# Layer 1's down-projection as seven products over both halves of the sequence, with its weights kept in SBUF

## The chip, the cores and the metric

One core of one Trainium2 chip. The metric is device time in microseconds (us) of one execution of the whole program; lower is better. The kernel before takes 2318.09 us, the median of 3 runs (2316.0 to 2323.02).

## What is computed

A trunk of two layers over a sequence of 1024 tokens of width 1024, then a final RMSNorm, all in float32. Layer 0 mixes with attention and spatial gating, layer 1 with a convolution. After each mixer comes a gated feed-forward, and the change is in the second of them:

```python
def conv_ffn(h, w_up, dw_w, dw_b, w_down):
    hh = causal_dwconv(h @ w_up, dw_w, dw_b)
    a, gate = jnp.split(hh, 2, axis=-1)
    return (a * jax.nn.silu(gate)) @ w_down
...
        x = x + conv_ffn(rms_norm(x, norm_ffn_g[l]), ffn_w_up[l], ffn_dw_w[l],
                         ffn_dw_b[l], ffn_w_down[l])
    return rms_norm(x, final_norm_g)
```

The hidden width is 2816, which is 22 tiles of 128. The down-projection of a layer is a product of 1024 tokens by 2816 by 1024.

## The kernel before

**Precision.** Every float32 operand of a matmul is split into a high and a low part (`split_hi_lo`, L138 to L144): ACT casts the high part (L140), POOL or DVE subtracts it for the low one (L144). Each product then takes three matmuls (`PASSES`, L157: high by high, high by low, low by high). A split operand is a buffer `hl` of 2 x 512 columns, of which the pool `whl` has 8; a raw operand of 1024 columns comes into one of 4 `raw` buffers (`wraw`).

**The sequence in two chunks.** Tokens are worked on in two chunks of 512 (`CH`). The residual stream of a chunk is one tile `xr` of 4 row tiles of 128.

**The up-projection** of a layer begins with plain products for the first hidden tiles (`head_steps`, L546), 8 of 22 in layer 1. Beside them `combos` (L578) makes sums and differences of the normed activations of both chunks. The other 14 tiles are made by `pair_steps` (L619): a step takes one hidden tile, its gate and its value, and computes both chunks' products with seven block products instead of eight (Strassen and Winograd's scheme, numbered 1 to 7; `product`, L638). A product is 12 matmuls. The seven weight operands of a step are sums of four quarters of weights, made by DVE (L662 to L665) and POOL (L667) and split by `part`. The products' banks are read by ACT copies (L676, L679, L682, L693) and DVE additions (L684, L686, L689) into rows `rg` and `rv_`; `conv` (L646) runs the width-3 convolution on each (ACT L648, two DVE operations L650), ACT applies SiLU (L691), and DVE multiplies value by gate (L695). The gated unit of 128 x 1024 goes to DRAM (`phd`).

**The down-projection** (`down_steps`, L699) is plain. Per chunk and per half of the output columns, 11 groups `dp` of two hidden tiles run: each loads 512 KB of weights and 512 KB of gated units from DRAM, splits both, and issues 24 matmuls (L721) into 4 banks, one for each row tile of 128 tokens; the last two groups run together, bank by bank, 12 matmuls each, and DVE adds each bank to `xr` (L726). That is 44 groups and 1056 matmuls for a layer. The weights are read twice, once for each chunk.

**The order.** Each engine runs its own list of instructions in order. The lists come from a scheduler that may place an instruction earlier or later than the program text, as long as its data allow. In layer 1 the text runs `ffn_rest`, then loads `xr`, then `down_steps(1, 0)`, then `down_steps(1, 1)` interleaved with `final_steps(0)` (the last norm of chunk 0, L955 to L983, whose POOL multiplication is L974), then `final_steps(1)`. Loads and stores go by SP's queue.

Of the kernel before, what the change touches and what calls it, by code (L numbers as in the profile page):

```python
# [10 lines left out]
F32 = mybir.dt.float32  # L11
# [9 lines left out]
P = 128  # L21
S = 1024
# [23 lines left out]
ROWS = 5  # L46
PRE0, PRE0_LATE = 6, 2
PRE1, PRE1_LATE = 8, 2
DP = HT // 2
# [7 lines left out]
def trunk_kernel(ctx: ExitStack, tc: tile.TileContext, x, norm_mix_g, norm_ffn_g, ab_w_in, ab_w_out,  # L57
# [43 lines left out]
    def run(steps):  # L101
        for f in steps:
            f()
# [213 lines left out]
    phd = [dram.tile([P, HT, S], F32, name=f"phd{l}") for l in range(2)]  # L317
# [227 lines left out]

    def head_steps(l, c, hT, js):  # L546
# [31 lines left out]
    def combos(l, hT, up_pool):  # L578
# [4 lines left out]
        def f(k):  # L583
# [6 lines left out]
            for c in range(2):  # L590
                t = c * TPC + k
                xt = up_pool.tile([P, D], F32, tag="row", name="xa", bufs=ROWS)
# [26 lines left out]
    def pair_steps(l, hT, T, js, up_pool):  # L619
# [34 lines left out]
        def f(j):  # L654
# [16 lines left out]
            a4 = part(v2, "pool")  # L671
            rg, rv_ = row(), row()
# [23 lines left out]
            nc.sync.dma_start(out=phd[l][:, j, :], in_=yv)  # L696
        return [lambda j=j: f(j) for j in js]

    def down_steps(l, c):  # L699
# [4 lines left out]
        def f(half, dp):  # L704
            if dp == 0:
# [3 lines left out]
                                                      in_=phd[l][:, 2 * dp:2 * dp + 2, c * CH:(c + 1) * CH]), PH_ENGINES)  # L709
# [19 lines left out]
    def x_from(src):  # L729
# [3 lines left out]
        return f  # L733

# [48 lines left out]
    def const_steps():  # L783
        rv = lambda ap: ap.rearrange("(c p) -> c p", p=P)

        def taps(c):
# [31 lines left out]
    def ffn_rest(l, hT, pre):  # L818
        with tc.tile_pool(name=f"up{l}", bufs=1) as up_pool:
            first, last, T = combos(l, hT, up_pool)  # L820
            interleave(head_steps(l, 1, hT, range(pre)), first, 0.0, 0.6)
            run(last)
            run(pair_steps(l, hT, T, range(pre, HT), up_pool))

# [106 lines left out]
    for c in range(NCH):  # L931
# [20 lines left out]
    for c in range(NCH):  # L952
        x_from(xd[1])(c)
# [31 lines left out]
    run(down_steps(1, 0))  # L985
    interleave(down_steps(1, 1), final_steps(0), 0.0, 0.5)
    run(final_steps(1))
# [36 lines left out]
```

## Time and profile before

| | before |
|---|---|
| median of 3 runs | 2318.09 us (2316.0 to 2323.02) |
| the profiled execution | 2318.01 us, its span 2316.3 us |
| mean granted TensorE clock | 0.970 |
| PE busy | 2171.3 us, 94% of the span |
| DVE, ACT, POOL busy | 1598.2, 1130.6, 1124.9 us |
| layer 1's products of the up-projection, on the chain that ended last | 1798.73 to 2055.62 us |
| layer 1's down-projection | from 2055.62 us to about 2304 us |

The rows further down come from the one profiled execution. Times are us from the start of its span; the mean of a group is in ns. A line such as L721 is a line of the kernel as printed above. A timeline's row gives start, length, engine, line and the operation's output and inputs; a group's row gives the count, the busy time, the mean of one, and the idle time of the engine just before them.

### The profile page before, as it was taken

The page shows a single profiled execution, that of the slowest core. Times are in us where ns is not written, and L with a number is a line of the kernel's source. Part 1 is how long each engine was busy: PE and PEld are TensorE (multiplying, and loading weights), DVE is VectorE, ACT ScalarE, POOL GpSimd, SP SyncE. Part 2 cuts the span into 40 slices and gives each one's busy share as a digit, 9 for nine tenths or more (in the row PEclk, how much of TensorE's full clock was granted, in tenths as well). Part 3 has the DMA queues.
Part 4 walks back from the last instruction along what each step waited for, and adds up shares of the span by engine and source line. Part 5 has one row for each costly group of instructions (what it writes and reads, how often), then busy time and mean ns, then how long its engine had stood idle before and what let it go on. Part 6 is the DMA issues. An engine that isn't in the chain of part 4 may idle for free.

```text
span 2316.3 us, 28698 instructions
## 1 busy us (share of the span) xinstructions
PE 2171.3 (94%) x10014; PEld 1781.0 (77%) x10014; DVE 1598.2 (69%) x2654; ACT 1130.6 (49%) x1993; POOL 1124.9 (49%) x879
## 2 busy tenths in 40 slices
PE   8888979989999999999999969979989999999997
PEld 6677758778788888878887758857768888888786
DVE  6675747964876666665599969996576666665654
ACT  4344525742544444544556566555433544544444
POOL 3312311222645444545579827974543554445554
PEclk9989979999999999999999979979989999999999
DMA  7736545435532222365534522522532222265564
GB/s 238 212 97 208 169 150 186 156 96 169 165 98 89 84 82 82 108 228 199 183 110 127 155 73 84 153 72 102 182 116 94 73 85 93 75 221 194 193 223 146
DMA packets 304049, 322.49 MB, mean 139 GB/s; under 512 B 12060, under 2 KB 221216, under 8 KB 303392
## 3 DMA queue, kind: packets, MB, share of 16 engines
q1 hardware_dynamic: 298016, 305.97, 41.1%
q0 software_dynamic: 5888, 14.68, 2.0%
q8 instruction: 79, 1.29, 0.2%
q14 instruction: 66, 0.54, 0.1%
HBM read 266.08 MB, written 54.53 MB: 138 GB/s over the span
## 4 chain that ended last, share of the span: by engine, by line
PE 70%; DVE 17%; issue 4%; ACT 3%; POOL 3%; DMA 2%; SPq 0%; ACTq 0%; DVEq 0%; POOLq 0%
PE bank L642 25%; PE bank L721 15%; PE bank L302 13%; PE bank L265 12%; DVE sbank L866 5%; DVE hl L144 2%; DVE y L178 2%; POOL ap L863 1%; PE sbank L461 1%; POOL hl L144 1%; DVE xn L193 1%; ACT hl L140 1%; PE sbank L209 1%; PE bank L430 1%; PE sbank L609 1%
## 5 line engine op out<-in xcount | busy, mean ns | idle before, releaser
L144 POOL TENSOR_TENSOR hl<-raw,hl 128x512 fp32r<-128x512 f32 x544 | 796.2, 1483 | 619.4 <-ACT hl L140 590.8
L140 ACT CAST hl<-raw 128x512 fp32r<-128x512 f32 x792 | 454.7, 617 | 339.2 <-PE bank L721 162.0
L302 PE MATMUL bank<-big,hl 128*128 128x512 f32 x2112 | 499.6, 395 | 9.0 <-DVE big L221 3.0
L721 PE MATMUL bank<-hl 128*128 128x512 f32 x2112 | 489.2, 391 | 8.3 <-DVE hl L144 6.5
L721 PEld LDWEIGHTS bank<-hl 128*128 128x128 f32 x2112 | 393.9, 188 | 98.9 <-DVE hl L144 15.2
L302 PEld LDWEIGHTS bank<-big,hl 128*128 128x128 f32 x2112 | 396.5, 190 | 94.8 <-ACT big L220 4.9
L265 PE MATMUL bank<-hl,big 128*128 128x512 f32 x1728 | 427.2, 401 | 20.5 <-POOL hl L144 9.3
L144 DVE TENSOR_TENSOR hl<-raw,hl 128x512 fp32r<-128x512 f32 x248 | 276.1, 1139 | 197.9 <-ACT hl L140 197.5
L265 PEld LDWEIGHTS bank<-hl,big 128*128 128x128 f32 x1728 | 325.6, 192 | 91.3 <-POOL hl L144 9.9
L642 PE MATMUL bank<-big,hl 128*128 128x512 f32 x1440 | 345.5, 390 | 0.1
L642 PEld LDWEIGHTS bank<-big,hl 128*128 128x128 f32 x1440 | 269.8, 188 | 59.0 <-POOL hl L144 1.0
L650 DVE SCALAR_TENSOR_TENSOR s<-row,dw,s 128x1024 f32<-128x1024 f32 x120 | 198.2, 1652 | 156.9 <-ACT s L648 153.0
L642 PE MATMUL bank<-t,hl 128*128 128x512 f32 x1080 | 265.3, 392 | 0.0
L866 DVE SCALAR_TENSOR_TENSOR sbank<-yb,cw,sbank 128x512 f32<-128x512 f32 x352 | 247.8, 746 | 6.0 <-ACT sbank L855 3.3
L642 PEld LDWEIGHTS bank<-t,hl 128*128 128x128 f32 x1080 | 202.5, 188 | 44.2
L863 POOL TENSOR_TENSOR ap<-ap,pr 128x512 f32<-128x512 f32 x112 | 154.2, 1376 | 35.3 <-ACT ap L858 21.5
L140 ACT CAST hl<-s 128x512 fp32r<-128x512 f32 x90 | 55.9, 621 | 156.9 <-DVE s L665 96.3
L556 DVE SCALAR_TENSOR_TENSOR s<-bank,dw,s 128x510 f32<-128x510 f32 x112 | 83.5, 745 | 57.0 <-ACT s L553 55.5
L862 ACT ACTIVATE pr<-yb,cw 128x512 f32<-128x512 f32 x112 | 80.8, 723 | 71.9 <-POOL ap L863 71.7
L667 POOL TENSOR_TENSOR s<-raw,s 128x512 f32<-128x512 f32 x30 | 38.9, 1295 | 122.8 <-DVE hl L144 122.7
L630 POOL MEMSET row<- 128x2 f32 x60 | 6.0, 99 | 156.4 <-DVE s L650 110.7
L648 ACT ACTIVATE s<-row,dw 128x1024 f32<-128x1024 f32 x60 | 74.9, 1248 | 12.2 <-DVE row L689 10.0
(170 smaller groups left out, 2082.8 us busy)
## 6 DMA issues: line engine op xcount, KB each, us to landing
raw<-in_ffn_w_up SPq DMA_DIRECT2D x116, 512.0 KB, 4.3
raw<-in_ffn_w_down SPq DMA_DIRECT2D x88, 512.0 KB, 3.8
raw<-phd SPq DMA_DIRECT2D x88, 512.0 KB, 4.7
raw<-in_ab_w_in SPq DMA_DIRECT2D x64, 256.0 KB, 4.0
raw<-in_conv_w_in SPq DMA_DIRECT2D x32, 512.0 KB, 4.0
phd<-s SPq DMA_DIRECT2D x30, 512.0 KB, 2.6
qd<-s SPq DMA_DIRECT2D x32, 256.0 KB, 2.8
qk<-qd POOLq DMA_DIRECT2D x8, 1024.0 KB, 7.1
```

The source lines that it names most:

```text
L140: nc.scalar.copy(out=hl_hi, in_=raw)
L144: eng.tensor_sub(out=hl_lo, in0=raw, in1=hl_hi.bitcast(F32))
L265: nc.tensor.matmul(ps, lhsT=hT[c][:, sa, d, tok(t)], rhs=units[d][:, sw, :], start=(n == 0), stop=(n == 3 * DT - 1))
L302: nc.tensor.matmul(ps, lhsT=hv[d // 4][:, sw, d % 4, :], rhs=hT[:, sa, d, :], start=(n == 0), stop=(n == 3 * DT - 1))
L556: nc.vector.scalar_tensor_tensor(out=y[:, sh:], in0=ps[:, :CH - sh], scalar=dw[:, k, ct:ct + 1], in1=y[:, sh:], op0=ALU.mult, op1=ALU.add)
L642: nc.tensor.matmul(ps, lhsT=hv[:, sw, d, :], rhs=B[n](sa, d), start=(start and i == 0), stop=(i == 11), skip_group_check=True)
L648: nc.scalar.activation(out=y, in_=r[:, 2:], func=AF.Identity, scale=dw[:, 2, ct:ct + 1], bias=dw[:, 3, ct:ct + 1])
L650: nc.vector.scalar_tensor_tensor(out=y, in0=r[:, k:k + S], scalar=dw[:, k, ct:ct + 1], in1=y, op0=ALU.mult, op1=ALU.add)
L721: nc.tensor.matmul(ps, lhsT=phs[i][:, sa, k * P:(k + 1) * P], rhs=wds[i][:, sw, :], start=(dp == 0 and n == 0), stop=(dp == DP - 1 and n = ...
L862: nc.scalar.activation(out=pr, in_=ys[ct][:, k:k + CH], func=AF.Copy, scale=cw[:, ct, k:k + 1])
L863: nc.gpsimd.tensor_add(out=st["ap"], in0=st["ap"], in1=pr)
L866: nc.vector.scalar_tensor_tensor(out=st["acc"], in0=ys[ct][:, k:k + CH], scalar=cw[:, ct, k:k + 1], in1=st["acc"], op0=ALU.mult, op1=ALU.add)
```

## The change

Layer 1's down-projection becomes `down_pair_steps`. Its hidden tiles are paired, `jj` with `HH + jj` (`HH` is 11). With the two chunks and the two column halves that makes blocks of 2 x 2 x 2, and each pair goes through the seven products. A product's unit for one pair is 3 matmuls for each of 4 row tiles: 12 matmuls, and 7 x 11 x 12 = 924 in all. Each of the four weight quarters of a pair (128 x 512) is loaded once and stays in SBUF, in `wraw`, in `big` and in a pool of its own; the weight operands of products 5, 3 and 7 are sums, for 3 and 7 made in place. The gated units' operands are kept in DRAM as seven slots `phs`. `sums` makes the three that are not plain, in the up-projection, as soon as both tiles of a pair exist; for this the pair steps go in the order k, HH + k, and the end of a pair (`finish`) is put into the next step, behind its weight splits. The products run in the order 2, 1, 5, 3, 6, 7, 4, into two sets of 4 banks, and at a product's end each bank is added to `xr` for each output block that it is part of. A next quarter's load is held back by a DVE copy of one element until a unit is made. In both layers the `row` buffers go from 5 to 4, and `combos` takes one of its two tiles from `s4`. Layer 0's down-projection stays plain.

```diff
-ROWS = 5
+ROWS = 4
...
+    def sums(jj, a11, a21, a12, a22):
...
+        nc.gpsimd.tensor_add(out=s1, in0=a21, in1=a22)
+        nc.gpsimd.tensor_sub(out=a21, in0=a11, in1=a21)
+        nc.gpsimd.tensor_sub(out=s2_, in0=s1, in1=a11)
+        s4_ = s2([P, CH])
+        nc.vector.tensor_sub(out=s4_, in0=a12, in1=s2_)
+        nc.sync.dma_start(out=phs[:, 4:6, jj, :], in_=sx)
+        nc.sync.dma_start(out=phs[:, 6, jj, :], in_=s4_)
...
             a4 = part(v2, "pool")
+            settle()
             rg, rv_ = row(), row()
...
-            nc.sync.dma_start(out=phd[l][:, j, :], in_=yv)
+            if l == 0:
+                nc.sync.dma_start(out=phd[:, j, :], in_=yv)
+            elif j < HH:
+                pair["a"] = yv
+            else:
+                pending.append(lambda: finish(j - HH, pair["a"], yv))
...
+        def weight(n, jj):
+            if n == 2:
+                place(jj)
+                load(2, jj)
+            (b11, b12), (b21, b22) = [(w[:, :512], w[:, 512:]) for w in W[jj]]
+            if n == 5:
+                t1 = s2([P, 512])
+                nc.vector.tensor_sub(out=t1, in0=b12, in1=b11)
+                return t1
+            if n == 3:
+                nc.gpsimd.tensor_sub(out=b12, in0=b22, in1=b12)
+                nc.vector.tensor_add(out=b11, in0=b11, in1=b12)
+            if n == 7:
+                nc.gpsimd.tensor_sub(out=b21, in0=b21, in1=b11)
+            return {3: b22, 2: b21, 1: b11, 6: b11, 7: b12, 4: b21}[n]
...
+            nc.sync.dma_start(out=raw[:, :len(js), :], in_=phs[:, SLOT[n], js[0]:js[-1] + 1, :])
+            us = []
+            for i, jj in enumerate(js):
+                us.append((unit(weight(n, jj), "pool"), unit(raw[:, i, :], "dve")))
+                if n in (2, 1, 5):
+                    load({2: 1, 1: 5, 5: 3}[n], jj, us[-1][1][:, 1, 0:1].bitcast(F32))
+            for grp in [us] if end else [[u] for u in us]:
+                for k in range(TPC):
...
+                    if end:
+                        for r, h in ADDS[n]:
+                            xt = xtile(r_tile(n, k))[:, h * 512:(h + 1) * 512]
+                            nc.vector.tensor_add(out=xt, in0=ps[k], in1=xt)
...
+        ds = down_pair_steps(1, dpool)
+        k = 5 * len(ds) // 7
+        run(ds[:2])
+        settle()
+        run(ds[2:4])
+        for c in range(NCH):
+            x_from(xd[1])(c)
+        run(ds[4:k])
+        interleave(ds[k:], final_steps(0), 0.0, 0.8)
+        run(final_steps(1))
```

The order of instructions on three lists, before and in the change. In the changed kernel L146 is the old L144, L663 is L630, L683 is L650, L695, L697, L698 and L700 are L662, L664, L665 and L667, L718, L720 and L723 are L684, L686 and L689, L729 is L695, and L1110 is L974. L553 to L557 are `sums`, L784 and L787 the in-place weight sums of products 3 and 7. A name with a number is one buffer.

DVE in the pair stage of layer 1, from the addition behind product 2 of one step to the weight sums of a later step, before:

```order
L689 TENSOR_TENSOR row<-bank,s_15737 128x512
L650 SCALAR_TENSOR_TENSOR s_15807<-row,dw_440,s_15807 128x1024 x2
L650 SCALAR_TENSOR_TENSOR s_15825<-row,dw_440,s_15825 128x1024
L662 TENSOR_TENSOR s_15977<-raw 128x512
L650 SCALAR_TENSOR_TENSOR s_15825<-row,dw_440,s_15825 128x1024
L664 TENSOR_TENSOR raw<-raw 128x512
L144 TENSOR_TENSOR hl<-s_15977,hl 128x512
L695 TENSOR_TENSOR s_15825<-s_15825,s_15807 128x1024
L684 TENSOR_TENSOR row<-bank,s_15907 128x512
L665 TENSOR_TENSOR s_15977<-s_15977,raw 128x512
```

and in the change, for the second tile of a pair:

```order
L723 TENSOR_TENSOR row<-bank,s_15634 128x512
L683 SCALAR_TENSOR_TENSOR s_15704<-row,dw_440,s_15704 128x1024 x2
L683 SCALAR_TENSOR_TENSOR s_15722<-row,dw_440,s_15722 128x1024 x2
L729 TENSOR_TENSOR s_15722<-s_15722,s_15704 128x1024
L557 TENSOR_TENSOR s_15762<-s_15722,sx 128x512
L723 TENSOR_TENSOR row<-bank,s_15785 128x512
L695 TENSOR_TENSOR s_15882<-raw 128x512
L697 TENSOR_TENSOR raw<-raw 128x512
L146 TENSOR_TENSOR hl<-s_15882,hl 128x512
L698 TENSOR_TENSOR s_15882<-s_15882,raw 128x512
```

The multiplication (old L695, now L729) was followed by the next step's split and additions, and the later step's weight sum (old L662) stood ahead of it. Now L557 stands right behind the multiplication, and behind L557 come a step's addition L723 and the weight sums L695 and L697 of the step after next.

POOL in the pair stage, before:

```order
L630 MEMSET row 128x2 x2
L667 TENSOR_TENSOR s_17113<-raw,s_17113 128x512
L144 TENSOR_TENSOR hl<-s_17113,hl 128x512
L144 TENSOR_TENSOR hl<-raw,hl 128x512 x3
L630 MEMSET row 128x2
```

and in the change:

```order
L700 TENSOR_TENSOR s_15731<-raw,s_15731 128x512
L146 TENSOR_TENSOR hl<-s_15731,hl 128x512
L146 TENSOR_TENSOR hl<-raw,hl 128x512 x4
L663 MEMSET row 128x2 x2
L553 TENSOR_TENSOR sx<-s_15581,s_15722 128x512
L554 TENSOR_TENSOR s_15581<-s_15581 128x512
L555 TENSOR_TENSOR sx<-sx,s_15581 128x512
L700 TENSOR_TENSOR s_15882<-raw,s_15882 128x512
L146 TENSOR_TENSOR hl<-s_15882,hl 128x512
```

The three sums L553 to L555 stand between the splits of one step and L700 of the step behind it.

POOL in the down-projection: before, its list there holds splits alone, 88 of them, and the 10 multiplications L974. In the change, from product 5's first splits of a sum to product 3's units:

```order
L146 TENSOR_TENSOR hl<-s_17998,hl 128x512
L146 TENSOR_TENSOR hl<-s_18022,hl 128x512
L784 TENSOR_TENSOR w_17488<-w_17489,w_17488 128x512
L1110 TENSOR_TENSOR xr<-xr,gain 128x512
L784 TENSOR_TENSOR w_17512<-w_17513,w_17512 128x512
L146 TENSOR_TENSOR hl<-s_18032,hl 128x512
L787 TENSOR_TENSOR w_17489<-w_17489,w_17488 128x512
L146 TENSOR_TENSOR hl<-s_18068,hl 128x512
L787 TENSOR_TENSOR w_17513<-w_17513,w_17512 128x512
L146 TENSOR_TENSOR hl<-s_18078,hl 128x512
L784 TENSOR_TENSOR wb<-wb 128x512 x2
L146 TENSOR_TENSOR hl<-s_18114,hl 128x512
```

The first two rows are splits of product 5's weight sums. Between each two splits stand one to three in-place sums of products 3 and 7, 22 of them down to the split of product 3's last units.

## Rows read from the trace of the kernel before

**Rows 1.** Page: busy time of each engine, share of the span, instructions.

```profile
PE 2171.3 (94%) x10014; PEld 1781.0 (77%) x10014; DVE 1598.2 (69%) x2654; ACT 1130.6 (49%) x1993; POOL 1124.9 (49%) x879
```

**Rows 2.** Chain that ended last, layer 1's feed-forward: start, length, engine, tile, line.

```profile
1798.73 256.89 PE bank L642 x1124
2055.62 5.48 PE bank L721 x24
2061.10 2.72 PE bank L642 x12
...
2205.34 94.85 PE bank L721 x417
```

**Rows 3.** Windows: busy of PE, PEld, DVE, ACT, POOL; PEclk, DMA share, GB/s.

```profile
1680.00:1700.00 20.00, 11.18 (x32) 8.46 (x33) 15.95 (x16) 2.85 (x4) 4.79 (x4) 0.66 0.20 68
1700.00:1720.00 20.00, 20.00 (x100) 16.60 (x100) 15.16 (x21) 9.83 (x17) 13.08 (x10) 1.00 0.40 119
1900.00:1950.00 50.00, 50.00 (x221) 41.09 (x220) 31.36 (x33) 26.38 (x40) 27.45 (x23) 1.00 0.25 81
```

**Rows 4.** Timeline of the end: the last matmuls and the last residual addition.

```profile
2295.71 7.87 PE L721 MATMUL bank<-hl 128*128 128x512 f32 x34
...
2305.69 0.68 DVE L726 TENSOR_TENSOR xr<-bank,xr 128x512 f32<-128x512 f32 x1
```

**Rows 5.** Windows of 5 us beside the first final steps.

```profile
2185.00:2190.00 5.00, 3.26 (x15) 2.37 (x14) 4.79 (x17) 4.46 (x10) 2.17 (x3) 1.00 0.36 109
...
2200.00:2205.00 5.00, 3.89 (x18) 2.88 (x16) 0.00 (x0) 1.47 (x3) 1.65 (x2) 1.00 1.04 392
```

**Rows 6.** Groups by line, pair stage of layer 1, 1800 to 2040 us.

```profile
L650 DVE SCALAR_TENSOR_TENSOR s<-row,dw,s 128x1024 f32<-128x1024 f32 x49 | 81.7, 1666 | 70.4 <-ACT s L648 70.0
L648 ACT ACTIVATE s<-row,dw 128x1024 f32<-128x1024 f32 x25 | 31.2, 1249 | 4.7 <-DVE row L689 4.7
...
L140 ACT CAST hl<-s 128x512 fp32r<-128x512 f32 x38 | 23.6, 621 | 71.8 <-DVE s L665 44.6 <-POOL s L667 17.4 <-DVE s L662 9.8
L144 DVE TENSOR_TENSOR hl<-s,hl 128x512 fp32r<-128x512 f32 x26 | 19.1, 734 | 3.3 <-ACT hl L140 2.5
...
L667 POOL TENSOR_TENSOR s<-raw,s 128x512 f32<-128x512 f32 x13 | 16.8, 1295 | 57.0 <-DVE hl L144 57.0
L695 DVE TENSOR_TENSOR s<-s,s 128x1024 f32<-128x1024 f32 x12 | 14.6, 1216 | 0.0
```

**Rows 7.** Timelines of ACT and DVE: from product 4's copy to the gated unit.

```profile
1910.25 0.59 ACT L693 COPY row<-bank 128x512 f32<-128x512 f32 x1 [2.56 <-PE bank L642]
...
1912.57 1.29 DVE L650 SCALAR_TENSOR_TENSOR s<-row,dw,s 128x1024 f32<-128x1024 f32 x1 [5.97 <-ACT s L648]
...
1916.77 1.22 DVE L695 TENSOR_TENSOR s<-s,s 128x1024 f32<-128x1024 f32 x1
```

**Rows 8.** Timelines of POOL and DVE in the down-projection.

```profile
2098.79 1.74 POOL L144 TENSOR_TENSOR hl<-raw,hl 128x512 fp32r<-128x512 f32 x1
2102.98 3.00 POOL L144 TENSOR_TENSOR hl<-raw,hl 128x512 fp32r<-128x512 f32 x2 [2.44 <-ACT hl L140]
...
2099.31 1.77 DVE L144 TENSOR_TENSOR hl<-raw,hl 128x512 fp32r<-128x512 f32 x1
2103.97 2.55 DVE L144 TENSOR_TENSOR hl<-raw,hl 128x512 fp32r<-128x512 f32 x2 [2.89 <-ACT hl L140]
```

**Rows 9.** Page, DMA issues: count, KB each, us from issue to landing.

```profile
raw<-phd SPq DMA_DIRECT2D x88, 512.0 KB, 4.7
```

**Rows 10.** Groups by line, down-projection, 2070 to 2160 us.

```profile
L144 POOL TENSOR_TENSOR hl<-raw,hl 128x512 fp32r<-128x512 f32 x35 | 53.7, 1555 | 34.9 <-ACT hl L140 34.9
L144 DVE TENSOR_TENSOR hl<-raw,hl 128x512 fp32r<-128x512 f32 x36 | 46.4, 1327 | 40.3 <-ACT hl L140 40.3
```

**Rows 11.** Timeline of PE ahead of layer 1's feed-forward.

```profile
1678.35 1.03 PE L217 MATMUL bank<-ident,xn 128*128 128x128 f32 x8
1684.74 1.94 PE L217 MATMUL bank<-ident,xn 128*128 128x128 f32 x8 [5.35 <-DVE big L221]
```

More of the change, by code (lines that the diff above doesn't have):

```diff
@@ L45 @@
 WHL = 8
-ROWS = 5
+ROWS = 4
 PRE0, PRE0_LATE = 6, 2
 PRE1, PRE1_LATE = 8, 2
+HH = HT // 2
+SLOT = {1: 0, 7: 1, 2: 2, 4: 3, 5: 4, 6: 5, 3: 6}
 DP = HT // 2
@@ L316, in trunk_kernel @@
     xd = [dram.tile([S, D], F32, name=f"xd{l}") for l in range(2)]
-    phd = [dram.tile([P, HT, S], F32, name=f"phd{l}") for l in range(2)]
+    phd = dram.tile([P, HT, S], F32, name="phd")
+    phs = dram.tile([P, 7, HH, CH], F32, name="phs")
     rn = [const.tile([P, NT], F32, name=f"rn{l}") for l in range(2)]
@@ L591, in f @@
                 t = c * TPC + k
-                xt = up_pool.tile([P, D], F32, tag="row", name="xa", bufs=ROWS)
+                xt = s4([P, D]) if c else up_pool.tile([P, D], F32, tag="row", name="xa", bufs=ROWS)
                 nc.sync.dma_start(out=xt, in_=xd[l][t * P:(t + 1) * P, :])
@@ L695, in f, with finish @@
             nc.vector.tensor_tensor(out=yv, in0=yv, in1=yg, op=ALU.mult)
-            nc.sync.dma_start(out=phd[l][:, j, :], in_=yv)
-        return [lambda j=j: f(j) for j in js]
+            if l == 0:
+                nc.sync.dma_start(out=phd[:, j, :], in_=yv)
+            elif j < HH:
+                pair["a"] = yv
+            else:
+                pending.append(lambda: finish(j - HH, pair["a"], yv))
+        def finish(jj, ya, yb):
+            nc.sync.dma_start(out=phs[:, 2:4, jj, :], in_=yb.rearrange("p (i c) -> p i c", i=2))
+            sums(jj, ya[:, :CH], ya[:, CH:], yb[:, :CH], yb[:, CH:])
+            nc.sync.dma_start(out=phs[:, 0:2, jj, :], in_=ya.rearrange("p (i c) -> p i c", i=2))
@@ L733, in x_from, with order @@
         return f
+    def order(l):
+        return list(range(HT)) if l == 0 else [j for k in range(HH) for j in (k, HH + k)]
     maskb = mp.tile([P, P], BF16, name="maskb")
@@ L820, in ffn_rest @@
             first, last, T = combos(l, hT, up_pool)
-            interleave(head_steps(l, 1, hT, range(pre)), first, 0.0, 0.6)
+            js = order(l)
+            interleave(head_steps(l, 1, hT, js[:pre]), first, 0.0, 0.6)
             run(last)
-            run(pair_steps(l, hT, T, range(pre, HT), up_pool))
+            run(pair_steps(l, hT, T, js[pre:], up_pool))
     ffn_rest(0, hF0, PRE0)
@@ L951, in trunk_kernel @@
     ffn_rest(1, hF1, PRE1)
-    for c in range(NCH):
-        x_from(xd[1])(c)
     def final_steps(c):
@@ L983, in final_steps @@
         return [lambda t=t: f(t) for t in range(c * TPC, (c + 1) * TPC)]
-    run(down_steps(1, 0))
-    interleave(down_steps(1, 1), final_steps(0), 0.0, 0.5)
-    run(final_steps(1))
+    with tc.tile_pool(name="down", bufs=1) as dpool:
+        ds = down_pair_steps(1, dpool)
[8 more added lines that the diff above has]
+        run(final_steps(1))
 _INS = ["x", "norm_mix_g", "norm_ffn_g", "ab_w_in", "ab_w_out", "diff_lq1", "diff_lk1", "diff_lq2", "diff_lk2",
```

77 lines of the change are left out of this document (71 added, 6 removed).

## Prediction

> **What bounds the kernel now.** I read the page first: PE is busy for 2171.3 us of the 2316.3 us span, 94%, and no other engine for more than 69% [rows 1]. The chain that ended last is PE's through the whole of layer 1's feed-forward: one piece of 1124 up-projection matmuls from 1798.73 to 2055.62, then the down-projection; the only other work in it is that of the pieces' joints [rows 2]. The windows show how full PE is: 50.00 us busy of 50 in the pair stage, with 221 matmuls [rows 3]. That gives the price of a matmul on the path, 50.00 / 221 = 0.2262 us; a group's mean of 390 ns is a matmul's latency, since matmuls overlap. The down-projection issues 1056 of them, from 2055.62 until 2295.71 + 7.87 = 2303.58 [rows 2, 4]; less 2.72 for 12 late matmuls of the up-projection inside [rows 2], it takes 245.2 us. At the full rate 1056 take 238.9, so 6.3 us are lost there. Part of it shows where the first final steps run beside it: PE busy 3.26 and 3.89 us in two windows of 5 [rows 5].
>
> The profiled execution took 2318.01 us, the median is 2318.09, so a sum from the trace needs no correction. About 0.3%, 7.0 us, is what a measurement of this kernel can tell from no change.
>
> **Matmuls: -29.9.** 924 instead of 1056, all on PE's path: 132 x 0.2262 = 29.9 us. Everything else in this change can only spend this gain or widen it by the 6.3 us.
>
> **Collision with the final steps: -2.8 (-6.3 to 0).** In the change the weights lie in SBUF by the time the final steps start, so the load behind the second window (DMA share 1.04 [rows 5]) goes, but the crowding of ACT and DVE (4.46 and 4.79 of 5 us in the first window) stays. I leave 3.5 of the 6.3.
>
> **Head steps and combos: 0 (0 to 4).** Four pairs are finished in the head steps, with 12 POOL sums and 4 DVE ones. POOL is busy 13.08 us of 20 there [rows 3], so the 12 x 1.3 = 15.6 us fit into idle time of the stretch; if one pair's sums alone stood in front of a combination that PE wants, 3 x 1.3 = 3.9 us. Fewer `row` buffers in both layers: a row is wanted again two steps later, some 38 us, and its convolution ends within 8 us of its step's end (shown below); 0. Were that cover gone, it would show as a wait of POOL's MEMSET on DVE.
>
> **Pair stage: +5 (0 to 21).** Here the order of instructions matters. A pair is 168 matmuls, 38.0 us. POOL gets three sums per pair (3.9 us at 1295 ns [rows 6]), DVE one (0.73). They are cheap; where they stand is the question. DVE's list now has L557 right behind the gated unit, and L557 waits for the three POOL sums, which wait for the unit. Queued behind L557 are L723, then the weight sums L695 and L697 for the second step of the next pair, on which that step's product 5 waits. From product 4's copy to the end of the gated unit took 1916.77 + 1.22 - 1910.25 = 7.7 us in one step [rows 7], with other DVE work in between; without, the copy (0.59), the activation L648 (1.25 [rows 6]), two L650 (1.29 each with no POOL beside), the multiplication (1.22) and the gaps between them need about 6.1. Then 3.9 for the sums, 0.73 for L557, two additions of 0.73, the cast 0.62 and the low part 0.73 [rows 6]: ready at 13.5 to 15.1, and with the sums at 1.74 [rows 8] at 16.5. PE wants it after the 67 matmuls that the scheduler has put between, 15.2 us. So a pair is between 1.7 us early and 1.3 us late; I take 0.7 late for each of 7 pairs, 5 us. The high end is DVE's list being full. It is busy 31.36 of 50 us [rows 3], 23.9 per 38.0, and idle for L648's sake 70.4 us in 240 [rows 6], 11.2 per pair. With the wait for the sums (3.9 to 5.2) and L557 that is 39.7 to 41.0 against 38.0: 3 x 7 = 21 us if none of the old idle time absorbs the new.
>
> **Start of the down-projection: +2 (0 to 6).** The first five units come through a tile of their own. The sixth, `ph`, lies in memory that the last pair's convolution still holds for about 6.7 us after product 4; then the load (4.7 to landing [rows 9]) and the split (0.62 + 0.73) make 12.7. PE has four units of 12 matmuls ahead of it, 10.9 us. Late by 2; with the split queued behind the last L557, by 6. The other loads stay ahead: 256 KB for a weight quarter instead of 512.
>
> **Products 5 and 3: +10.5 (3 to 19).** The 22 in-place sums on POOL (L784, L787) belong to products 3 and 7, but POOL's list has them all between product 5's second split and product 3's fourth, with 13 splits and one final multiplication: 36 operations. PE needs for that stretch, with the lead of three units that eight `hl` buffers allow, 16 units x 12 x 0.2262 = 43.4 us. A POOL operation of this size alone is 1.295 us [rows 6], a split beside one of DVE 1.74, two beside two of DVE 3.00 [rows 8], and the mean of the plain down-projection is 1555 ns [rows 10]. DVE has some 31 operations with two SBUF inputs in the same stretch, so I take the 1.50: 54.0, a stall of 10.5. At 1.295 it is 46.6, a stall of 3; at 1.74, 62.6, a stall of 19. In the plain down-projection POOL has 35 splits in 90 us and idles 34.9 of them [rows 10]; that slack is the cover, and it is gone for these 43 us. Here a rule of the Trainium skill speaks against the change.
>
> The page "SBUF — State Buffer", section "SBUF: two separate sides", says that DVE, in an operation with two SBUF inputs, and GpSimd shut each other out of a shared port pair for a whole instruction. The trace nearly agrees: two and two took 3.54 us from 2102.98 to 2106.52 [rows 8], against 2 x 1.295 + 2 x 0.73 = 4.05 one by one. By the full rule the stretch would take 36 x 1.295 + 31 x 0.73 = 69.3 us, the stall 26, and the sum 2320.
>
> **The tail: +2 (0 to 4).** A product ends bank by bank with 6 matmuls (1.36 us) each instead of 12, so the last four row tiles reach the final norm closer together; before, the last addition already started 2.1 us behind the last matmul [rows 4]. One more tile's worth of that is 2.
>
> **Sum.** 2318.0 - 29.9 - 2.8 + 5 + 2 + 10.5 + 2 = **2304.8 us**.
>
> **The rivals.** *Everything hides.* All terms at their low ends: 2318.0 - 29.9 - 6.3 + 3 = 2284.8, and a little of each left gives 2285 to 2297. For it: PE was busy throughout the pair stage, and POOL's operations can cost as little as 1.295 [rows 6]. Against it: POOL's 36 operations need more than PE's time even then. 0.15.
>
> *POOL and DVE take turns.* In the stretch of products 5 and 3 each pair of operations costs what one cost beside the other, 1.77 us [rows 8]: 31 x 1.77 + 5 x 1.295 = 61.3, a stall of 18, and the pair stage is late by 1.3 x 7 = 9. 2304.8 + 7.5 + 4 = 2316, no change that can be told. For it: both lists are dense there. Against: many of DVE's operations run early. 0.28 for 2311 to 2325. The page's rule, taken in full, ends in this case too.
>
> *Slower.* DVE's list in the pair stage is the one mechanism: L557 holds it for POOL, and each pair loses 3 us, 21 in all. After a wait of 5.35 us the next eight transposes of PE took 1.94 us where eight before it took 1.03 [rows 11], at a granted 0.66 in that stretch [rows 3], so a restart at the lower of the two levels (1.2 GHz) can cost about 1 us more per pair: 2304.8 - 5 + 21 + 7 = 2328. It decides the sign from 25 us, 3.6 per pair, on. Against it: much of DVE's idle time is slack that the new wait can use. 0.12.
>
> That the change doesn't do what it says has no room: the matmuls are counted in PE's list.
>
> **How the numbers follow.** Forecast 2304.8, the likeliest case, with 0.45 for 2297 to 2311. Faster by over 7.0 us (under 2311) is that and the hidden case, 0.60; within, 0.28; slower (over 2325), 0.12. The range leaves out the lower part of the hidden case and most of the slower one: 2290 to 2324.
>
> **What would show it.** The down-projection's line has 924 matmuls. In the pair stage PE waits for DVE's low part or ACT's cast of a sum, under 1.5 us a time. Between products 5 and 3 PE waits for POOL's split some 10 us in all, and POOL is over 90% busy. Waits on loads stay under 3 us. Wrong: PE fully busy through products 5 and 3 (POOL's stall never comes), or gaps of 3 us or more in every pair (DVE's list), or a granted clock under 1.00 in the pair stage.

## The result and the profile after

The changed kernel takes 2340.68 us, the median of 4 runs (2339.47 to 2343.59), against 2318.56 for the kernel before; the ratio is 1.0095, with a 95% interval of 1.0076 to 1.0114. It is slower by about 22 us, 1%, where 2304.8 was forecast and 2324 was the end of the range. The profiled execution took 2339.52 us with a span of 2337.6.

The page's first part answers to [rows 1]: PE is busy 12 us less, and its span is 21 us longer.

```profile
PE 2158.9 (92%) x9882; PEld 1763.6 (75%) x9882; DVE 1675.2 (72%) x2721; ACT 1120.9 (48%) x1971; POOL 1198.4 (51%) x923
```

The longest waits of PE from the end of the head steps on (us in all, times, longest); the kernel before waited 4.0 us in all from there on:

```profile
PE sbank L819 <- POOL hl L146: 9.8, 8, 3.7
PE bank L675 <- DVE row L720: 8.2, 5, 2.2
PE sbank L819 <- ACT hl L142: 8.1, 1, 8.1
PE bank L675 <- ACT hl L142: 6.9, 3, 6.0
PE bank L819 <- DVE xr L826: 2.3, 1, 2.3
```

Where they lie shows in the windows of the changed kernel (columns as in [rows 3]): ahead of the pair stage, the pair stage, the wait at the start of the down-projection, the rest of products 2 and 1, products 5 and 3, and all that follows.

```profile
1793.26:1799.31 6.05, 0.01 (x1) 0.00 (x0) 3.25 (x6) 1.79 (x4) 3.85 (x4) 0.92 0.42 158
1799.31:2086.70 287.39, 277.07 (x1177) 222.76 (x1178) 207.36 (x188) 132.59 (x199) 166.38 (x128) 0.98 0.32 103
...
2097.70:2105.77 8.07, 0.00 (x1) 0.00 (x1) 0.71 (x2) 0.67 (x2) 3.26 (x3) 0.78 1.02 404
2105.77:2153.64 47.87, 47.87 (x205) 39.49 (x205) 37.19 (x52) 21.13 (x39) 26.78 (x19) 0.97 0.77 262
2153.64:2209.42 55.78, 43.64 (x161) 32.14 (x159) 50.08 (x43) 15.78 (x29) 55.78 (x35) 0.91 0.35 106
2209.42:2324.90 115.48, 114.60 (x502) 93.62 (x500) 76.34 (x100) 55.67 (x110) 68.97 (x50) 1.00 0.32 97
```

A matmul at full speed costs 0.2272 us in both traces (94.85 / 417 in the chain of before; the estimate of 0.2262 was 0.4% low). I cut both traces at the same two points, the end of the last transposes of the combinations and the end of the last up-projection matmul; between them lie 1176 matmuls in each (1152 of the up-projection and 24 of the down-projection before, 1164 and 12 after, since 12 of the up-projection fewer stand ahead of the first point).

| us | before | after | difference |
|---|---|---|---|
| start to the last transposes | 1794.7 | 1793.3 | -1.5 |
| from there to the last up-projection matmul | 269.1 | 293.5 | +24.4 |
| from there to the last matmul (1032 and 912 matmuls) | 239.8 | 238.0 | -1.7 |
| from there to the end of the span | 12.7 | 12.8 | 0.0 |

So the 120 matmuls fewer of the third line, 27.3 us, were given back almost entirely inside the down-projection, and the up-projection ahead of it became 24 us longer, though PE has the same number of matmuls there.

**The pair stage.** DVE's timeline of one pair (start, length, idle before), then POOL's beside it:

```profile
1895.13 0.69 DVE L557 TENSOR_TENSOR s<-s,sx 128x512 f32<-128x512 f32 x1 [4.03 <-POOL sx L555]
1895.74 0.68 DVE L723 TENSOR_TENSOR row<-bank,s 128x512 f32<-128x512 f32 x1
1896.34 0.68 DVE L695 TENSOR_TENSOR s<-raw 128x512 f32<-128x512 f32 x1
...
1905.13 1.78 DVE L695 TENSOR_TENSOR s<-raw 128x512 f32<-128x512 f32 x1
...
1908.55 1.78 DVE L146 TENSOR_TENSOR hl<-s,hl 128x512 fp32r<-128x512 f32 x1
...
1893.80 1.30 POOL L555 TENSOR_TENSOR sx<-sx,s 128x512 f32<-128x512 f32 x1
1900.59 1.30 POOL L700 TENSOR_TENSOR s<-raw,s 128x512 f32<-128x512 f32 x1 [5.49 <-DVE hl L146]
...
1904.09 5.69 POOL L146 TENSOR_TENSOR hl<-raw,hl 128x512 fp32r<-128x512 f32 x3
```

L557 does hold DVE, 4.03 us in each pair. But two other things stand in the rows: the weight sum L695 took 0.68 us at 1896.34, where POOL was idle, and 1.78 at 1905.13, where POOL split without a pause; and the low part (L146) behind it took 1.78 too. From 1805 to 2040 us the group means are:

```profile
L146 DVE TENSOR_TENSOR hl<-s,hl 128x512 fp32r<-128x512 f32 x24 | 22.5, 939 | 9.5 <-ACT hl L142 9.0
...
L698 DVE TENSOR_TENSOR s<-s,raw 128x512 f32<-128x512 f32 x12 | 14.1, 1177 | 0.4
...
L557 DVE TENSOR_TENSOR s<-s,sx 128x512 f32<-128x512 f32 x5 | 3.5, 693 | 20.1 <-POOL sx L555 20.1
```

DVE's operations became longer, while the additions that read a bank (in PSUM) stay at 0.68. POOL's too: of its operations from 1800 to 2080 us, 49 began while DVE was idle or in such an addition and took 1.28 to 1.31 us each, and 18 began inside one of DVE's 128x512 operations on SBUF alone and took 1.67 to 1.76 (the other 35 began in one of 128x1024). The waits that end on PE are mostly for L720, an addition that frees a bank and comes late since DVE's list is late; I had expected them at product 5.

Idle time is only half of what PE lost. It was busy for 277.07 of the stage's 287.39 us; 1177 matmuls at 0.2272 would need 267.4, so 9.7 us went into matmuls that followed each other more slowly. The granted clock of the stage is 0.98. Behind the wait of 6.0 us it stood at the lower of the two levels (1.2 GHz) from 1798.4 to 1805.2, where 14 matmuls kept PE busy for 5.89 us, 0.42 each, and it was there again from 1962.2 to 1965.6; that explains some 4 of the 9.7 us, an estimate from the 21 matmuls that began at this level at 0.2 us more each.

**Products 5 and 3.** Here POOL is busy for 55.78 us of 55.78 and DVE for 50.08. Their timelines, side by side, show why; first DVE, then POOL:

```profile
2173.59 1.77 DVE L785 TENSOR_TENSOR wb<-wb 128x512 f32<-128x512 f32 x1
...
2175.35 1.72 DVE L781 TENSOR_TENSOR s<-wl 128x512 f32<-128x512 f32 x1
2176.99 1.77 DVE L146 TENSOR_TENSOR hl<-ph,hl 128x512 fp32r<-128x512 f32 x1
```

```profile
2173.08 1.74 POOL L146 TENSOR_TENSOR hl<-s,hl 128x512 fp32r<-128x512 f32 x1
2174.77 1.75 POOL L784 TENSOR_TENSOR wb<-wb 128x512 f32<-128x512 f32 x1
2176.48 3.40 POOL L787 TENSOR_TENSOR wb<-wb 128x512 f32<-128x512 f32 x2
```

Each of POOL's operations takes 1.7 us, where 1.295 was one alone, and each of DVE's that reads SBUF alone takes 1.7, where 0.73 was the mean in the old pair stage [rows 6]. Both lists advance by one operation per 1.7 us, one of each: the engines seem to take turns. PE idled for 12.1 of the 55.78 us; the rest of what it lost, 7.1 us, lies in its 161 matmuls, at a granted 0.91 (43.64 us busy, 36.6 at full speed). POOL had no pause, so I take its list for what set the length.

**The start.** The sixth unit's load was issued at 2095.94, when the last convolution ended, and ACT got it at 2105.10; the 2 MB load of the residual stream had been issued 2.9 us ahead of it, and the DMA engines were busy throughout PE's wait (share 1.02 in the window above):

```profile
2093.04 0.39 SPq L867 DMA_DIRECT2D xr<-xd  x1
...
2095.94 0.88 SPq L808 DMA_DIRECT2D ph<-phs  x2
...
2105.10 0.62 ACT L142 CAST hl<-ph 128x512 fp32r<-128x512 f32 x1 [12.61 <-DMA ph<-phs]
```

### The profile page after: what moved, and what is told of

Its sections match the earlier page's. It is cut to its first block, busy times and chain, and to the rows that moved or that the text cites. A ratio compares the mean times of both kernels' runs of the same rounds, so it can differ in the third digit from the quotient of the medians.

```text
span 2337.6 us, 28662 instructions
## 1 busy us (share of the span) xinstructions
PE 2158.9 (92%) x9882; PEld 1763.6 (75%) x9882; DVE 1675.2 (72%) x2721; ACT 1120.9 (48%) x1971; POOL 1198.4 (51%) x923
## 3 DMA queue, kind: packets, MB, share of 16 engines
q8 instruction: 78, 1.28, 0.2%
## 4 chain that ended last, share of the span: by engine, by line
PE 58%; DVE 23%; issue 7%; POOL 5%; ACT 5%; DMA 2%; SPq 0%; ACTq 0%; POOLq 0%; DVEq 0%
PE bank L675 15%; PE bank L304 14%; PE bank L267 11%; PE bank L856 6%; PE bank L819 5%; DVE sbank L1004 5%; DVE s L683 3%; DVE hl L146 3%; POOL hl L146 2%; DVE y L180 1%; POOL ap L1001 1%; ACT s L681 1%; PE sbank L464 1%; PE sbank L819 1%; ACT hl L142 1%
## 5 line engine op out<-in xcount | busy, mean ns | idle before, releaser
L146 POOL TENSOR_TENSOR hl<-raw,hl 128x512 fp32r<-128x512 f32 x456 | 671.7, 1491 | 510.4 <-ACT hl L142 486.4
L142 ACT CAST hl<-raw 128x512 fp32r<-128x512 f32 x616 | 357.6, 617 | 228.5 <-PE bank L856 64.5
L683 DVE SCALAR_TENSOR_TENSOR s<-row,dw,s 128x1024 f32<-128x1024 f32 x120 | 198.1, 1651 | 123.3 <-ACT s L681 106.7
L856 PE MATMUL bank<-hl 128*128 128x512 f32 x1056 | 247.7, 392 | 4.3 <-DVE hl L146 3.9
L146 DVE TENSOR_TENSOR hl<-raw,hl 128x512 fp32r<-128x512 f32 x160 | 170.9, 1088 | 90.3 <-ACT hl L142 90.1
L856 PEld LDWEIGHTS bank<-hl 128*128 128x128 f32 x1056 | 196.2, 188 | 51.3 <-DVE hl L146 11.0
L819 PE MATMUL bank<-hl 128*128 128x512 f32 x726 | 176.4, 394 | 3.1 <-DVE xr L826 2.3
L819 PEld LDWEIGHTS bank<-hl 128*128 128x128 f32 x726 | 137.7, 190 | 33.9 <-DVE xr L826 2.7
L142 ACT CAST hl<-s 128x512 fp32r<-128x512 f32 x101 | 62.7, 621 | 163.0 <-DVE s L698 87.5
L146 DVE TENSOR_TENSOR hl<-ph,hl 128x512 fp32r<-128x512 f32 x72 | 101.9, 1428 | 44.8 <-ACT hl L142 44.8
```

Source lines behind the costliest of these rows:

```text
L142: nc.scalar.copy(out=hl_hi, in_=raw)
L146: eng.tensor_sub(out=hl_lo, in0=raw, in1=hl_hi.bitcast(F32))
L683: nc.vector.scalar_tensor_tensor(out=y, in0=r[:, k:k + S], scalar=dw[:, k, ct:ct + 1], in1=y, op0=ALU.mult, op1=ALU.add)
L819: nc.tensor.matmul(ps[k], lhsT=a[:, sa, k * P:(k + 1) * P], rhs=w[:, sw, :], start=(n in (5, 2, 1) and js[0] == 0 and i == 0), stop=(end a ...
L856: nc.tensor.matmul(ps, lhsT=phs[i][:, sa, k * P:(k + 1) * P], rhs=wds[i][:, sw, :], start=(dp == 0 and n == 0), stop=(dp == DP - 1 and n = ...
```

## The experiments

Times of single runs are near 2319 for the kernel before. The end of the last transposes, up to which all these kernels do the same work (v7 and v8 nearly so), lay between 1787.8 and 1798.7 us in the different traces, so the totals carry some 10 us that have nothing to do with the edits, and a single run's total inside an expected range says little. I therefore compare the two stretches of the table above, "pairs" (changed kernel 293.5, before 269.1) and "down" (238.0; before 239.8 for 120 matmuls more). In v7 and v8 12 matmuls more stand ahead of the first point, and 2.7 us are added for them.

| kernel | time | pairs | down |
|---|---|---|---|
| changed | 2340.68 | 293.5 | 238.0 |
| no_pair_sums | 2323.42 | 277.3 | 238.2 |
| l557_pool | 2329.79 | 286.7 | 237.9 |
| rows5 | 2340.22 | 293.4 | 239.1 |
| reload_b21 | 2336.36 | 293.5 | 236.5 |
| dve_single | 2331.23 | 293.5 | 233.8 |
| early7_x1 | 2342.22 | 293.4 | 239.2 |
| late3 | 2338.21 | 294.0 | 230.1 |
| v4 | 2329.39 | 286.7 | 230.7 |
| v5 | 2329.90 | 284.0 | 239.0 |
| v6 | 2328.82 | 281.9 | 244.8 |
| v7 | 2317.15 (10 runs) | 285.9 | 221.5 |
| v8 | 2317.74 | 291.7 | 220.5 |

My theory after the result: in the pair stage the sums on POOL hold DVE's list, and in products 5 and 3 the lists of POOL and DVE need more than PE's time. The rivals: the fewer row buffers or the new order of tiles; and a limit that POOL and DVE share, which no move of work from one to the other, or to a neighbouring place, would lift.

**no_pair_sums** leaves the sums of the pair stage out:

```diff
-            sums(jj, ya[:, :CH], ya[:, CH:], yb[:, :CH], yb[:, CH:])
+            nc.sync.dma_start(out=phs[:, 4:6, jj, :], in_=ya.rearrange("p (i c) -> p i c", i=2))
+            nc.sync.dma_start(out=phs[:, 6, jj, :], in_=yb[:, :CH])
```

> The four sums at the end of each of the 7 pairs of the pair stage are left out; their three slots are written with plain gated units by the same DMAs, so the output is not the reference's. If the sums cost the pair stage its 21 us, it falls from 287.4 to 266 to 271 us and the time to 2316 to 2323. If the new order of the tiles, the later end of a pair or the fewer row buffers cost it, the stage stays over 278 us.

"Pairs" fell by 16.2 us, to 277.3, of which 6.0 are still the wait ahead of the stage; the stage itself took 271.3. The waits for L720 are gone, and the groups are back:

```profile
L146 DVE TENSOR_TENSOR hl<-s,hl 128x512 fp32r<-128x512 f32 x24 | 17.2, 716 | 5.7 <-ACT hl L142 5.1
...
L698 DVE TENSOR_TENSOR s<-s,raw 128x512 f32<-128x512 f32 x12 | 9.2, 769 | 0.1
```

So the 18 operations on POOL and 6 on DVE that lie in the stage (the seventh pair's come behind it) cost 16 us: not by their own length on DVE (6 x 0.7 us), but by what they do to the others. The new tile order and the later end of a pair cost some 2 us at most (271.3 against 269.1).

**rows5** sets `ROWS` to 5.

> The row buffers go back from 4 to 5, all else as changed. If DVE's list is the cause of the pair stage's loss, nothing changes: stage within 3 us of 287.4, time within 4 of 2339.5. If PE's waits for DVE's L720 (8.2 us, 5 times) come from rows that are freed late, the stage falls by 5 us or more.

Nothing changed (293.4): the row buffers are not it.

**l557_pool** moves one operation:

```diff
-        nc.vector.tensor_sub(out=s4_, in0=a12, in1=s2_)
+        nc.gpsimd.tensor_sub(out=s4_, in0=a12, in1=s2_)
```

> The last of the four sums of a pair (L557) goes from DVE to POOL, so that DVE's list no longer waits for POOL there. If DVE's list being held is what lengthens the pair stage, the wait of 4.03 us per pair on DVE disappears, the pair stage (287.4 us in the changed kernel, 1799.3 to 2086.7) falls to 279 us or less, PE's wait of 6.0 us ahead of it falls to under 2, and the profiled execution (2339.5) to 2320 to 2330. If it is the sum of the work of DVE and POOL on their shared port, which only changes engine here, the stage stays within 3 us of 287 and the time within 4 of 2339.

"Pairs" fell by 6.8 us, and the wait ahead of the stage from 6.0 to 2.8 and 1.5, so the stage itself took 282.4 and missed the 279. The time fell into its range with the help of 2.8 us that this run was ahead at the last transposes; the 9.7 us that the expectations of v4 and v8 below give for the stage contain them. The wait of DVE is gone, but its operations grew further, since DVE now works where it had waited, beside POOL:

```profile
L146 DVE TENSOR_TENSOR hl<-s,hl 128x512 fp32r<-128x512 f32 x24 | 28.6, 1193 | 6.3 <-ACT hl L142 5.8
...
L698 DVE TENSOR_TENSOR s<-s,raw 128x512 f32<-128x512 f32 x12 | 19.0, 1583 | 0.4
...
L557 POOL TENSOR_TENSOR s<-s,sx 128x512 f32<-128x512 f32 x5 | 8.1, 1618 | 0.4
```

That is the miss that mattered: with L557 away from DVE, L698 went from 1177 to 1583 ns (769 without sums), and L557 itself took 1618 on POOL. Each theory had a part. The held list was worth 6.8 us, 5.1 of them in the stage. The stage is still 11.1 us longer than without sums; that the shared limit costs these is argued from the longer operations, and no run changes it alone in this stage.

**dve_single** measures that limit. DVE's 22 weight sums read one column instead of a second full operand:

```diff
-                nc.vector.tensor_sub(out=t1, in0=b12, in1=b11)
+                nc.vector.tensor_scalar_add(out=t1, in0=b12, scalar1=b11[:, 0:1])
...
-                nc.vector.tensor_add(out=b11, in0=b11, in1=b12)
+                nc.vector.tensor_scalar_add(out=b11, in0=b11, scalar1=b12[:, 0:1])
```

> DVE's 22 weight sums of products 5 and 3 (L781, L785) read one full operand and one column of the other instead of two full operands; lists and counts stay nearly the same, so the output is not the reference's. In the changed kernel both engines are without a pause in that stretch, POOL at 1.67 to 1.74 us an operation and DVE at 1.61 to 1.75, as if each operation waited for one of the other engine. If operations with two SBUF inputs on DVE and operations on POOL take turns, these 22 go to about 0.7 us, POOL's mean falls to 1.5 or less, and the stretch loses 10 us or less instead of 19; time 2328 to 2333. If POOL is simply slow and its 36 operations are the bound, POOL's mean stays over 1.65 and the loss over 15.

The first row below is the operation with POOL idle (min, median and max of two: 475 to 486 ns); then one of DVE beside POOL, and three of POOL: one that began while DVE was in an operation with two full operands, one that began in the operation of the row above, and one that began in an addition that reads a bank:

```profile
L781 DVE TENSOR_SCALAR s<-w x2: 475/480/486, 2120.2 to 2122.8; 128x512 f32<-128x512 f32 x2
...
2174.76 1.32 DVE L785 TENSOR_SCALAR wb<-wb 128x512 f32<-128x512 f32 x1
...
2174.07 1.73 POOL L787 TENSOR_TENSOR wb<-wb 128x512 f32<-128x512 f32 x1
2175.76 1.48 POOL L784 TENSOR_TENSOR wb<-wb 128x512 f32<-128x512 f32 x1
...
2188.21 1.28 POOL L146 TENSOR_TENSOR hl<-w,hl 128x512 fp32r<-128x512 f32 x1
```

On DVE 0.48 us became 1.3 to 1.5 in most of them, so the expected 0.7 was wrong: an operation with one full operand waits for POOL as well. All of POOL's operations from 2145 to 2200 us fall into these three kinds: 15 that began in a two-operand operation of DVE took 1.70 to 1.75 us, 15 that began in a one-operand operation 1.44 to 1.49, and 5 that began while DVE was idle or in an addition that reads a bank 1.27 to 1.30. What they lose follows the length of DVE's operation, and neither list alone is the bound: each engine waits, nearly for the whole of it, for the operation that the other has begun. I call this the exclusion. "Down" fell by 4.2. The same 161 matmuls of products 5 and 3 lost 14.0 us instead of 19.7 (counted from the first to the next behind them), between the two expectations; the time came into its range only because this run was 4.8 us ahead at the last transposes.

The Trainium skill, page "SBUF — State Buffer", section "SBUF: two separate sides", describes such a lock: whichever starts first, a GpSimd operation or one of DVE with two SBUF inputs or in a 2-port mode, has a shared port pair for the whole instruction. The trace nearly agrees: one by one a pair would take 1.295 + 0.73 = 2.0 us (an estimate), and the trace has 1.7.

**reload_b21** takes 11 of POOL's 36 operations out of the stretch, by a second load of b21 that arrives during product 3:

```diff
-                if n in (2, 1, 5):
-                    load({2: 1, 1: 5, 5: 3}[n], jj, us[-1][1][:, 1, 0:1].bitcast(F32))
+                if n in (2, 1, 5, 3):
+                    load({2: 1, 1: 5, 5: 3, 3: 2}[n], jj, us[-1][1][:, 1, 0:1].bitcast(F32))
```

> The fourth weight quarter is loaded a second time during product 3, held back by a one-element copy, so that the 11 sums of product 7 (L787) cannot stand on POOL's list among the splits of products 5 and 3; POOL then has 25 operations there instead of 36. If POOL's list is the bound there, the stretch from product 5's first matmul to the end of product 3 (55.8 us for 161 matmuls, 19 us lost) loses 6 us or less and the time falls by 11 to 15. If the loss comes from DVE's additions and splits or from the port, of which DVE's part stays as it is, it still loses 14 or more.

A gain of 1.5 us only; the same 161 matmuls still lost 16.1 us, the second case of the expectation. POOL's waits shrank, and a longer one for DVE came in their place: the additions to `xr` of product 5 stand behind the sums on DVE's list, and product 3 needs their banks.

```profile
2192.23 1.75 DVE L785 TENSOR_TENSOR wl<-wl 128x512 f32<-128x512 f32 x1
...
2193.96 1.27 DVE L826 TENSOR_TENSOR xr<-sbank,xr 128x512 f32<-128x512 f32 x2
...
2194.78 4.55 PE L819 MATMUL sbank<-hl 128*128 128x512 f32 x12 [5.46 <-DVE xr L826]
```

**late3** takes all in-place sums out of products 5 and 3 (product 5's own sum L781 on DVE stays): it reloads b12 during product 3 and b21 during product 6, and moves L784 and L785 to product 6.

```diff
-            if n == 3:
+            if n == 6:
                 nc.gpsimd.tensor_sub(out=b12, in0=b22, in1=b12)
                 nc.vector.tensor_add(out=b11, in0=b11, in1=b12)
...
+                if n in (2, 1, 5, 3, 6):
+                    load({2: 1, 1: 5, 5: 3, 3: 5, 6: 2}[n], jj, us[-1][1][:, 1, 0:1].bitcast(F32))
```

> All in-place weight sums are moved out of products 5 and 3: quarter b12 is loaded again during product 3 and b21 during product 6, held back by one-element copies, and the sums of product 3 are written with product 6, which is the first to need them. POOL and DVE then have 11 sums each beside product 6 and POOL 11 beside product 7. If the lists are too full only because the sums stand so early, products 5 and 3 run without a wait over 1 us, the 33 sums fit beside products 6, 7 and 4 (55 POOL operations at 1.7 us are 93 us against 90 us of matmuls and the lead), and the down-projection from the last up-projection matmul to its last (238.0 us in the changed kernel) falls to 220 to 227 us; time 2324 to 2330. If the loss follows the work wherever it stands, products 6 and 7 lose what 5 and 3 gain, and it stays over 232 us.

"Down" fell by 7.9 to 230.1, between the two expectations. The 161 matmuls of products 5 and 3 lost 0.8 us; the 502 behind them lost 11.0 instead of 1.6, so half of the gain came back as loss there, and the start's wait was 9.1 this time:

```profile
PE sbank L819 <- ACT hl L142: 9.7, 2, 9.1
PE bank L819 <- POOL hl L146: 4.3, 4, 2.0
```

**early7_x1** lengthens the tile `early` (`js[0] < 7` instead of 5) and loads the second half of the residual stream after five more steps.

> The tile of its own for the first gated units of product 2 holds 7 of them instead of 5, and the second half of the residual stream is loaded behind more of the steps, after the first load into the tile that waits for the convolution's memory. If PE's wait of 8.1 us at the start comes from that one late load (issued at 2095.9 when the last convolution ended, landed some 9 us later, against 4.5 for the median), PE wants it 5.4 us later and it lands sooner, so the wait falls under 2 us and the time to 2329 to 2332. If the wait is one for DVE or POOL, behind the last pair's sums, it stays over 5 us.

The wait stayed at 8.3 us, but in another place. From SP's timeline, then ACT's:

```profile
2098.26 0.33 SPq L808 DMA_DIRECT2D ph<-phs  x1
...
2107.83 0.33 SPq L559 DMA_DIRECT2D phs<-s  x1
2111.20 1.91 SPq L808 DMA_DIRECT2D ph<-phs  x4
...
2102.21 0.62 ACT L142 CAST hl<-ph 128x512 fp32r<-128x512 f32 x1 [5.04 <-DMA ph<-phs]
...
2117.69 0.62 ACT L142 CAST hl<-ph 128x512 fp32r<-128x512 f32 x1 [13.30 <-DMA ph<-phs]
```

The load that had been late now landed in 4 us, with nothing large just ahead of it. The next ones were issued only at 2111.20: on SP's queue they stand behind the last store of the last pair's sums (L559, 2107.83), and SP then waited 3.0 us more for a store to `phs` to land. Two causes lay in a row, and taking the first one away let the second one show.

**v4** puts late3, l557_pool and early7_x1 together, stores a pair's last plain slots as soon as they exist, and puts the last pair's sums behind the loads of five steps of product 2. **v5** and **v6** also make the sums of the last 3 or 4 pairs in the down-projection, from DRAM:

```diff
+        oa, ob = s4([P, S]), s4([P, S])
+        nc.sync.dma_start(out=oa.rearrange("p (i c) -> p i c", i=2), in_=phs[:, 0:2, jj, :])
+        nc.sync.dma_start(out=ob.rearrange("p (i c) -> p i c", i=2), in_=phs[:, 2:4, jj, :])
+        sums(jj, oa[:, :CH], oa[:, CH:], ob[:, :CH], ob[:, CH:])
+        nc.sync.dma_start(out=phs[:, 1, jj, :], in_=oa[:, CH:])
```

> Four edits together: the weight sums late (as late3), L557 on POOL (as l557_pool), seven units in the tile of their own with the second residual load later (as early7_x1), and the last pair's plain slots stored at once, its sums behind the loads of product 2. Measured alone: l557_pool's pair stage with the wait ahead of it was 9.7 us shorter. If the causes add up, the time is 2308 to 2318, and PE's wait at the start of the down-projection under 4 us. If the start only waits at the next load (as in early7_x1, where the next loads stood behind the last pair's stores on SP's queue), that wait stays at 6 us or more and the time at 2316 to 2324.

> v4, and the sums of the last 3 pairs are made in the down-projection beside products 2 and 1, from the plain slots in DRAM. If it is the sums' place that costs the pair stage about 2.5 us a pair, the last three pairs run at 38.2 us as before the change, the stage gains 6 to 9 us on v4, the start's wait falls under 3 us as nothing stands between the last pair and the loads, and the time is 2298 to 2308, faster than both kernels. If DVE and POOL are full beside products 2 and 1 too (22 splits each and now 12 sums in 60 us), the gain comes back as waits there, and the time is within 4 us of v4.

> v5 with 4 pairs instead of 3. If the place is what costs, another 2 to 3 us less than v5. If products 2 and 1 have no more room on POOL, 1 to 5 us more than v5.

In v4 the gains of the two stretches add up (286.7 and 230.7), but the start's wait stayed, at 8.2 us, and the time missed both of its ranges; the run was 4.1 us behind the changed kernel at the last transposes, which explains a part. In v5 and v6 the hoped-for case failed and the other one came: the pairs gained 2.7 and 4.8 us on v4, and the down-projection lost 8.3 and 14.1. v6's longest waits there:

```profile
PE sbank L829 <- ACT hl L142: 11.6, 3, 7.3
PE bank L829 <- POOL hl L146: 6.8, 7, 1.9
```

So the work of DVE and POOL can't be put beside products 2 and 1 for nothing; how much of this loss is the exclusion and how much the added loads was not taken apart.

**v7** reorders the steps, so that PE has other units while the last pair's slots are stored, and lets the sums of the last head pair wait for the first pair step:

```diff
+        ds = ds[:5] + ds[6:11] + [ds[5], ds[11]] + ds[12:]
...
+                if 2 * jj + 2 == PRE1:
+                    pending.append(rest)
+                else:
+                    rest()
```

**v8** is v7 with L557 on DVE.

> v4 with two edits of order: the units of product 1 for pairs 0 to 8 stand ahead of the last two pairs of product 2, so that PE has some 24 us more work before it needs what the last pair of the up-projection stores; and the sums of the last pair of the head steps wait for the first pair step instead of standing in front of its weight sums. If the wait at the start (8.2 us in v4) is one for the last pair's stores and the loads queued behind them, it falls under 2 us, and the wait ahead of the pair stage (2.8 + 2.0 in v4) under 2; from the last transposes of the combinations to the last matmul it then takes 503 to 509 us (v4 517.4, the kernel before 511.6), and the time is 2308 to 2316, the first version faster than the kernel before. If the room on DVE and POOL is what bounds the stage, the waits come back elsewhere and the stretch stays over 513.

> v7 with the fourth sum L557 on DVE again. In l557_pool the pair stage with the wait ahead of it was 9.7 us shorter than in the changed kernel; if 5 of these were the wait ahead of the stage, which v7 removes in another way, v8 loses 3 to 6 us against v7.

The wait at the start is gone, and "down" fell from 230.7 to 221.5. From the last transposes to the last matmul v7 takes 507.4 us, inside the expected 503 to 509; the kernel before takes 511.6 by the same count (269.1 + 239.8, and 2.7 for 12 matmuls of the up-projection that stand ahead of its first point too), 4.2 us more. The median of 10 runs is 2317.15 us against 2319.56 for 13 runs of the kernel before; the ratio is 0.9988, with an interval of 0.9975 to 1.0001. That is no difference that can be told, above the 2308 to 2316 expected. v8's stretches are 4.8 us longer together, within its expectation. What v7 still waits for:

```profile
PE bank L681 <- DVE row L726: 7.8, 4, 2.2
PE bank L825 <- POOL hl L146: 5.1, 6, 2.0
PE bank L681 <- ACT hl L142: 3.4, 1, 3.4
```

The wait ahead of the pair stage fell only from 4.8 to 3.4, not under 2, and the L720 waits (L726 here) stay.

## Why the prediction was wrong

- **Matmuls, -29.9:** right. 924 were issued, and 0.2272 instead of 0.2262 makes it 30.0.
- **Collision, -2.8:** inside its range. At 0.2272 the old down-projection lost 5.3 us (245.2 - 1056 x 0.2272); the last 502 matmuls now lose 1.4 (115.48 us), which makes it -3.9.
- **Tail, +2:** 0.0.
- **Head steps, 0 (0 to 4):** 6.0. The case that I named, one pair's sums ahead of what PE wants, happened; behind them stood L557, the weight sums and the cast.
- **Pair stage, +5 (0 to 21):** 18.4 beyond that wait, inside the range but not for its reason. The failed step is "They are cheap; where they stand is the question": I priced DVE's operations behind the sums at 0.73 us, the mean of a stage in which POOL was often idle. With the sums both lists work at the same time more often, and the same operations took 0.94 to 1.18 us in the mean. The held list, on which my high end rested, was worth 5.1 us of the 18.4, the new order and the rest some 2, and 11.1 stay with the sums wherever L557 runs. These I put down to the exclusion; that is argued, not isolated. An estimate by rows says the same: from 1800 to 2040 us of the kernel before, POOL's 79 operations at 1.29 and DVE's on SBUF alone (49 L650 at 1.28, 12 L695 at 1.22, 63 others at 0.69) make 223 us one by one, 93% of the time; a pair's sums add 4.6, which makes 39.9 us of 38.0. It is somewhat high, since a pair of operations takes 1.7 and not 2.0.
- **Start, +2 (0 to 6):** 8.1 and a slower restart. The failed step is the load at 4.7 us: it landed after some 9, behind 2 MB of residual stream on the same queue. The convolution also let go of the memory 9.1 us after product 4 (2086.8 to 2095.9), not 6.7.
- **Products 5 and 3, +10.5 (3 to 19):** 55.78 us for 161 matmuls, 19.2 lost. The failed step is the choice of 1.50 us from two operations beside two. There the engines began and ended alone; in two lists without a pause every operation has a partner, and the row of one beside one (1.74) was the right one.
- **The signs:** PE's waits for POOL's split were 9.8 us and POOL was busy throughout, as forecast, but 2.3 us of waits for DVE and 7.1 us in slower matmuls came on top. Two signs spoke against the forecast: a load that cost PE over 3 us, and a granted clock of 0.98 in the pair stage. A pair took 41.7 us there instead of some 38.
- **The range:** "POOL and DVE take turns" (0.28) and "slower" (0.12) were set up as rivals, each against the forecast in the other places. They came together: the stall of 18 of the first and, by luck, about the 21 of the second, whose mechanism, the held list, gave only 5.1 of them. 2318.0 - 29.9 - 4 + 6.0 + 18.4 + 9.4 + 19.2 = 2337.1 (9.4 is the start's wait and 1.3 of slow restart), against 2339.5 measured; 1.3 of the difference lie ahead of the last transposes, where 12 matmuls (2.7 us) are gone and only 1.5 us were gained.

## What to carry to other kernels

Before giving idle time of two engines to new work, ask whether the two can use it at the same time: here POOL at 49% and DVE at 69% looked free, but beside each other their 128 x 512 operations cost 1.7 us a pair, and by the estimate above the pair stage was 93% full for the two together. Price an operation by the rows in which the other engine is busy throughout, if that is what the new lists will look like. And when rivals do not shut each other out, let them come together in one case of the range.

## What was not expected of the hardware

A DVE operation with one full float32 operand (0.48 us alone) also waits for POOL, and took up to 1.57 us; a 128x512 addition that reads one operand from PSUM did not, at 0.66 to 0.70 in every trace from 1780 us on, and POOL's operations that began in one stayed at 1.28 to 1.31. After the wait of 8.1 us at the start, PE's first 4 matmuls took 2.07 us; the granted clock stood at the lower level from 2102.2 to 2109.0. In products 5 and 3, with waits of up to 3.7 us, it was there twice more, and the stretch was granted 0.91.
